# The score products of two query blocks taken together, their second halves on 64 rows of the array each

## Chip, cores and metric

The kernel runs on one core of a Trainium2 chip. The metric is device time in microseconds (us) of one execution. TensorE does the matrix products, ScalarE (ACT) the activations and copies with a scale, VectorE (DVE) the element-wise work and the scans, GpSimd (POOL) small odd jobs, and SyncE (SP) issues most of the DMA transfers.

## What is computed

A transformer block over 2048 tokens of width 1024. Half of its mixing is stick-breaking attention with 8 heads of 64 channels, the other half is a gated unit; an MLP of width 4096 follows. The change touches the scores `z` of the attention and the store of the queries that feed them.

```python
def stick_breaking_attention(q, k, v):
    # A[t,s] = sigmoid(z_ts) * prod_{s<j<t} (1 - sigmoid(z_tj)), z = q.k / sqrt(Dh)
    for blk in range(s // Q_BLOCK):                 # 128 queries at a time
        qb, kb, vb = qh[:, :, q0:kv_len], kh[:, :, :kv_len], vh[:, :, :kv_len]
        z = jnp.einsum('bhqd,bhkd->bhqk', qb, kb) * scale
        causal = s_idx < t_idx
        log_keep = jnp.where(causal, jax.nn.log_sigmoid(-z), 0.0)
        suffix = lax.cumsum(log_keep, axis=3, reverse=True) - log_keep
        a = jnp.where(causal, jnp.exp(jax.nn.log_sigmoid(z) + suffix), 0.0)
        outs.append(jnp.einsum('bhqk,bhkd->bhqd', a, vb))

x = x + concat(rmsnorm(attention), rmsnorm(gated)) @ w_out
x = x + square(relu(rmsnorm(x) @ w_up)) @ w_down
return rmsnorm(x)
```

## The kernel before

The products are wanted at float32 accuracy, but run in the faster form float32r. So an operand is split by `split` (L85, L86 or L88, L89) into a high part, a rounded copy made by ACT, and a low part, the rest, made by DVE. A product of two split operands is then high x high + high x low + low x high: `mm3` (L93, L94, L95), three matmuls of 512 columns each.

The scores are made in another way. A head has 64 channels, half of the 128 rows of the array, so the tile `qt` holds the high parts of the queries in rows 0 to 63 and their low parts in rows 64 to 127, while `kt` holds the keys twice, once in each half of the rows: `kt[:, 0]` the high parts, `kt[:, 1]` the low parts. One matmul over 128 rows with `kt[:, 0]` gives high x high and low x high together (L370), and one with `kt[:, 1]` gives high x low and low x low (L371).

The tokens are cut in 4 chunks of 512 (`c`) and these in 4 blocks of 128 queries (`tb`). A unit of the attention is one chunk of queries, one head and one segment of 512 keys (`seg`); there are 80 units and so 320 steps. A step (`weigh`) makes the scores `z` of one query block against up to 512 keys in one of two buffers of the accumulation memory (pool `ps_z`); on the diagonal (`seg == c`, 128 of the steps) the keys are 256, 256, 384 and 512 and a small matmul adds the mask (L373). ACT reads `z` twice (`kk` L377, `b` L379), DVE runs the scan along the keys (L382, L385) and multiplies (L383, L386). Five steps later `turn` transposes `b` on TensorE (L396) and splits it (`aT`, L85, L86), and two steps after that `gather` multiplies it with the values (L414, L415).

The attention is a generator, `side`. The helper `together` runs it beside the main work: one step for each step of the projections of chunks 2 and 3, then half a step for each step of the output projection and of the first MLP half. Where the main work needs a finished chunk of the attention, the attention runs alone until that chunk is there (`while steps[0] < ...: next(side)`). After the attention's end the kernel has the rest of the MLP alone. The order of each engine's instructions is set at build time, by a scheduler that goes by a simulated time line; so an edit in one place can move instructions in others.

The queries come from `transposed_cols(0, q_d)`: 16 results of 128 x 512 are split with one ACT and one DVE instruction each (L88, L89), and stored to `q_d` with two transfers each (L208); `qt` is loaded from there, once for each chunk and head (L359).

Of the kernel before, what the change touches and what calls it, by code (L numbers as in the profile page):

```python
# [8 lines left out]
F32 = mybir.dt.float32  # L9
F32R = mybir.dt.float32r  # L10
# [6 lines left out]
P = 128  # L17
D = 1024
T = 2048
NH = 8  # L20
HD = 64
SBW = 512
DFF = 4096
TC = 512
# [4 lines left out]
QK_SCALE = 0.125  # L29
# [5 lines left out]
def block_kernel(ctx: ExitStack, tc: tile.TileContext, x, x_t, gmix, w_in, ln_g, ln_b, sgw, sgb,  # L35
                 outg, w_out, gmlp, w_up, w_down, gfin, out):
    nc = tc.nc
    const = ctx.enter_context(tc.tile_pool(name="const", bufs=1))
    dram = ctx.enter_context(tc.tile_pool(name="dram", bufs=1, space=DRAM))
# [4 lines left out]
    ident_b = const.tile([P, P], BF16, name="ident_b")  # L44
# [5 lines left out]
    neg_b = const.tile([P, P], BF16, name="neg_b")  # L50
# [12 lines left out]
    nc.gpsimd.memset(mone, -1.0)  # L63


    q_d = dram.tile([NH, 2, HD, T], F32, name="q_d")
    k_d = dram.tile([NH, 2, HD, T], F32, name="k_d")
    v_d = dram.tile([NC, NH, P, NTB, 2, HD], F32, name="v_d")
    a_d = dram.tile([SBW, T], F32, name="a_d")
# [12 lines left out]
    def split(hi, lo, src, scale=None):  # L82

        if scale is None:
            nc.scalar.activation(hi, src, AF.Copy)  # L85
            nc.vector.tensor_tensor(lo, src, hi.bitcast(F32), ALU.subtract)  # L86
        else:
            nc.scalar.activation(hi, src, AF.Copy, scale=scale)  # L88
            nc.vector.scalar_tensor_tensor(lo, src, scale, hi.bitcast(F32), ALU.mult, ALU.subtract)  # L89
# [23 lines left out]
    def proj(cs, places, sp, gated_first, staging):  # L113
# [32 lines left out]
        def weights(col):  # L146
            if col in ready:
                return ready.pop(col)
            return [weight(col, k2) for k2 in range(KD // 2)]
# [37 lines left out]
        def transposed_cols(col, dst):  # L187
            ws = weights(col)
            for ci, (c, pl) in enumerate(zip(cs, places)):
                for e in range(4):  # L190
                    es = slice(e * P, (e + 1) * P)
                    ps = pl.ps()
                    for k in range(KD):
                        w, h = ws[k // 2], hT[ci][k // 2]
                        mm3(ps, w[:, 0, k % 2, es], w[:, 1, k % 2, es], h[:, 0, k % 2, :], h[:, 1, k % 2, :],
                            k == 0, k == KD - 1)
                        if k == 3:
                            yield
                    st = sp.tile([P, 2, TC], F32R, name="qkv_st", bufs=2)
                    if col == 0:  # L200

                        split(st[:, 0, :], st[:, 1, :], ps, QK_SCALE)
                    else:
                        t = sp.tile([P, TC], F32, name="gelu_t", bufs=3)
                        nc.vector.tensor_tensor(t, ps, r_rows[ci], ALU.mult)
                        split(st[:, 0, :], st[:, 1, :], t)
                    for j in range(2):
                        nc.sync.dma_start(dst[2 * e + j, :, :, c * TC:(c + 1) * TC].rearrange("x d t -> d x t"),  # L208
                                          st[j * HD:(j + 1) * HD].bitcast(F32))
                    yield  # L210

        def natural(col, evac):
# [128 lines left out]
    def attention(cs):  # L341

        units = [(c, h, seg) for c in cs for h in range(NH) for seg in range(c, -1, -1)]
        state = {}

        def weigh(u, tb):
            c, h, seg = units[u]
            diag = seg == c
            tcs = slice(c * TC, (c + 1) * TC)
            ss = slice(seg * TC, (seg + 1) * TC)  # L350
            if tb == 0:
                kt = att.tile([P, 2, TC], F32R, name="kt", bufs=2)
                for j in range(2):
                    nc.sync.dma_start(kt[j * HD:(j + 1) * HD].bitcast(F32), k_d[h, :, :, ss].rearrange("x d t -> d x t"))
                vt = att.tile([P, NTB, 2 * HD], F32R, name="vt", bufs=3)
                nc.sync.dma_start(vt.bitcast(F32), v_d[seg, h].rearrange("p n x d -> p n (x d)"))
                if diag:
                    qt = att.tile([P, TC], F32R, name="qt", bufs=2)
                    nc.sync.dma_start(qt.bitcast(F32), q_d[h].rearrange("x d t -> (x d) t")[:, tcs])  # L359
                    carry = [None] * NTB  # L360
                else:
                    qt, carry = state[u - 1][2:4]
                state[u] = [kt, vt, qt, carry, []]
            kt, _, qt, carry, bs = state[u]
            L = (tb + 1) * P if diag else TC
            z = ps_z.tile([P, TC], F32, name="z")
            ql = qt[:, tb * P:(tb + 1) * P]

            Z = max(L, 2 * P)
            nc.tensor.matmul(z[:, :Z], ql, kt[:, 0, :Z], start=True, stop=False)  # L370
            nc.tensor.matmul(z[:, :Z], ql, kt[:, 1, :Z], start=False, stop=not diag)  # L371
            if diag:
                nc.tensor.matmul(z[:, L - P:L], ident_b, neg_b, start=False, stop=True)  # L373
            row = c * NTB + tb
            kk = kks[kk_n[0] % NKK]
            kk_n[0] += 1
            nc.scalar.activation(kk[:, :L], z[:, :L], AF.Sigmoid, scale=rq[:, 1, row:row + 1])  # L377
            b = att.tile([P, TC], F32, name="b", bufs=9)
            nc.scalar.activation(b[:, :L], z[:, :L], AF.Sigmoid, scale=rq[:, 0, row:row + 1])  # L379
            pr = att.tile([P, TC + 1], F32, name="pr", bufs=5)  # L380
            if diag:
                nc.vector.tensor_tensor_scan(pr[:, L - 1::-1], kk[:, L - 1::-1], zeros[:, :L], 1.0, ALU.mult, ALU.add)  # L382
                nc.vector.tensor_tensor(b[:, :L - 1], b[:, :L - 1], pr[:, 1:L], ALU.mult)  # L383
            else:
                nc.vector.tensor_tensor_scan(pr[:, ::-1], kk[:, ::-1], zeros, carry[tb], ALU.mult, ALU.add)  # L385
                nc.vector.tensor_tensor(b, b, pr[:, 1:TC + 1], ALU.mult)  # L386
            carry[tb] = pr[:, 0:1]
            bs.append(b)

        def turn(u, j):  # L390
            c, h, seg = units[u]
            t0 = j * P if seg == c else 0
            bs = state[u][4]
            tr = ps_t.tile([P, TC], F32, name="tr")
            for tb in range(t0 // P, NTB):
                nc.tensor.transpose(tr[:, tb * P:(tb + 1) * P], bs[tb][:, j * P:(j + 1) * P], ident)  # L396
            aT = att.tile([P, 2, TC], F32R, name="aT", bufs=4)
            split(aT[:, 0, t0:], aT[:, 1, t0:], tr[:, t0:])
            if t0 > TC - 2 * P:
                t0 = TC - 2 * P  # L400
                nc.gpsimd.tensor_copy(aT[:, :, t0:t0 + P], zeros[:, :2 * P].rearrange("p (a b) -> p a b", a=2))
            state[u, j] = aT, t0

        heads = {}

        def gather(u, j):
            c, h, seg = units[u]
            first, last = seg == c and j == 0, seg == 0 and j == NTB - 1
            aT, t0 = state.pop((u, j))
            vt = state[u][1]  # L410
            if first:
                heads["av"] = ps_av.tile([P, TC], F32, name="av")
            av = heads["av"]
            nc.tensor.matmul(av[:, t0:], vt[:, j, :], aT[:, 0, t0:], start=first, stop=False)  # L414
            nc.tensor.matmul(av[:, t0:], vt[:, j, :], aT[:, 1, t0:], start=False, stop=last)  # L415
            if not last:
                return
            if h % 2 == 0:
                heads["ao"] = att.tile([P, TC], F32, name="ao", bufs=1)
            ao = heads["ao"]  # L420
            low = att.tile([HD, TC], F32, name="low", bufs=1)
            nc.scalar.activation(low, av[HD:2 * HD, :], AF.Copy)
            o0 = (h % 2) * HD
            nc.vector.tensor_tensor(ao[o0:o0 + HD, :], av[0:HD, :], low, ALU.add)
            if h % 2 == 1:
                nc.sync.dma_start(a_d[(h // 2) * P:(h // 2 + 1) * P, c * TC:(c + 1) * TC], ao)

        n = len(units) * NTB
        for i in range(n + DRAIN):
            if i < n:  # L430
                weigh(i // NTB, i % NTB)
            if 0 <= i - LATE < n:
                turn((i - LATE) // NTB, (i - LATE) % NTB)
            if i >= DRAIN:
                gather((i - DRAIN) // NTB, (i - DRAIN) % NTB)
            steps[0] = i + 1
            yield
# [550 lines left out]
    with ExitStack() as es:  # L988
        att = es.enter_context(tc.tile_pool(name="att", bufs=1, side="right", reuse_waits="tile"))
        ps_z = es.enter_context(tc.tile_pool(name="ps_z", bufs=2, space=PSUM, reuse_waits="tile"))  # L990
# [99 lines left out]
```

## Time and profile before

| what | value |
|---|---|
| median of 3 runs | 2500.56 us (2498.76 to 2502.59) |
| profiled execution, its own time | 2500.81 us |
| span from its first to its last instruction | 2499.1 us |
| granted TensorE clock, mean | 0.985 |
| TensorE matmul busy | 2427.0 us (97%) |
| DVE busy | 1686.5 us (67%) |
| ACT busy | 1197.9 us (48%) |

In the rows below PE is TensorE's matmuls, PEld its loads of the stationary operand (the weights) and SPq the queue in which SyncE issues transfers. L370 is line 370 of the kernel before. Busy times of PE are modelled ends of pipelined instructions and overlap: what a matmul takes from the engine is read from the distance between the starts of two that follow one another.

### The profile page before, as it was taken

The numbers are of one execution on the slowest core, as the hardware profiler recorded it, in microseconds if no ns is written. First come the engines' busy times: TensorE is split into PE (matmuls) and PEld (weight loads), VectorE is DVE, ScalarE is ACT, GpSimd is POOL, SyncE is SP. The second block draws the span as 40 slices with busy tenths as digits, with TensorE's granted clock in tenths as the row PEclk, the third lists the DMA queues.
The fourth block names the chain that finished last, engine by engine and source line by source line (L and its number), as shares of the span: only waits on it lengthen the run. The fifth ranks groups of instructions, "written<-read, shape, count | busy, mean of one in ns | idle before, by whom it ended". The sixth has DMA issues, their size and how long they took to land.

```text
span 2499.1 us, 30545 instructions
## 1 busy us (share of the span) xinstructions
PE 2427.0 (97%) x11424; PEld 1986.8 (79%) x11424; DVE 1686.5 (67%) x2264; ACT 1197.9 (48%) x2004; POOL 322.1 (13%) x288
## 2 busy tenths in 40 slices
PE   8999999998899999999999899999999999899998
PEld 7888788886687888888877688888888888688886
DVE  4752678865957666666668878744686666577788
ACT  5433457553736655655655545322244444433333
POOL 1110011000100000000000000000123222224432
PEclk9999999998999999999989999999999999999999
DMA  9788977668644334433364543353533444744422
GB/s 378 295 303 280 316 256 247 200 217 282 199 148 143 119 125 131 122 115 111 124 257 170 176 130 113 105 197 126 211 118 139 155 146 163 260 182 153 168 101 101
DMA packets 161108, 455.00 MB, mean 182 GB/s; under 512 B 13376, under 2 KB 29760, under 8 KB 141504
## 3 DMA queue, kind: packets, MB, share of 16 engines
q1 hardware_dynamic: 150320, 417.39, 49.3%
q0 software_dynamic: 6336, 33.56, 3.3%
q10 hardware_dynamic: 4304, 2.10, 0.3%
q8 instruction: 90, 1.47, 0.2%
q14 instruction: 58, 0.48, 0.1%
HBM read 322.97 MB, written 130.02 MB: 181 GB/s over the span
## 4 chain that ended last, share of the span: by engine, by line
PE 83%; DVE 8%; DMA 4%; issue 3%; ACT 2%; POOL 0%; SPq 0%; DVEq 0%; POOLq 0%; ACTq 0%
PE mm L94 23%; PE mm L95 23%; PE mm L93 23%; PE tr L396 4%; PE av L414 2%; PE av L415 2%; PE z L370 2%; PE z L371 2%; DVE w L86 2%; DMA v_d<-qkv_st 1%; DVE pr L385 1%; DMA w_in<-wi_d 1%; PE mm L524 1%; DVE t L86 1%; DVE aT L86 1%
## 5 line engine op out<-in xcount | busy, mean ns | idle before, releaser
L93 PE MATMUL mm<-t,t 128*128 128x512 f32 x1280 | 503.7, 395 | 1.4 <-DVE t L86 1.4
L95 PE MATMUL mm<-t,t 128*128 128x512 f32 x1280 | 503.1, 393 | 0.0
L94 PE MATMUL mm<-t,t 128*128 128x512 f32 x1280 | 501.8, 392 | 0.0
L377 ACT ACTIVATE kk<-z,rq 128x512 f32<-128x512 f32 (+2 forms) x320 | 201.7, 631 | 289.0 <-PE z L371 177.0
L385 DVE TENSOR_TENSOR_SCAN pr<-kk,pr,zeros 128x513 f32<-128x513 f32 x192 | 246.6, 1285 | 119.1 <-ACT kk L377 118.7
L93 PEld LDWEIGHTS mm<-t,t 128*128 128x128 f32 x1280 | 242.3, 189 | 52.0 <-DVE t L86 1.9
L95 PEld LDWEIGHTS mm<-t,t 128*128 128x128 f32 x1280 | 241.7, 189 | 51.8
L94 PEld LDWEIGHTS mm<-t,t 128*128 128x128 f32 x1280 | 242.0, 189 | 50.1
L85 ACT ACTIVATE aT<-tr 128x512 fp32r<-128x512 f32 (+1 forms) x320 | 172.1, 541 | 100.2 <-PE tr L396 99.5
L86 DVE TENSOR_TENSOR aT<-tr,aT 128x512 fp32r<-128x512 f32 (+1 forms) x320 | 190.7, 599 | 25.3 <-ACT aT L85 25.2
L396 PE MATMUL tr<-ident,b 128*128 128x128 f32 x1088 | 180.9, 279 | 24.2 <-DVE aT L86 21.9
L379 ACT ACTIVATE b<-z,rq 128x512 f32<-128x512 f32 (+2 forms) x320 | 201.0, 629 | 2.8 <-PE tr L396 2.7
L85 ACT ACTIVATE t<-t 128x1024 fp32r<-128x1024 f32 x104 | 104.5, 1059 | 170.4 <-DMA t<-in_w_down 101.3
L94 PE MATMUL mm<-w,w 128*128 128x512 f32 x448 | 176.3, 393 | 8.8 <-DVE w L86 8.6
L396 PEld LDWEIGHTS tr<-ident,b 128*128 128x128 f32 x1088 | 133.2, 143 | 60.7 <-DVE aT L86 30.4
L95 PE MATMUL mm<-w,w 128*128 128x512 f32 x448 | 175.1, 391 | 0.0
L85 ACT ACTIVATE w<-raw 128x512 fp32r<-128x512 f32 (+1 forms) x135 | 106.7, 802 | 140.4 <-PE mm L95 130.7
L382 DVE TENSOR_TENSOR_SCAN pr<-kk,zeros 128x128 f32<-128x128 f32 (+3 forms) x128 | 104.4, 818 | 92.0 <-ACT kk L377 91.8
L86 DVE TENSOR_TENSOR w<-raw,w 128x512 fp32r<-128x512 f32 (+1 forms) x135 | 149.9, 1112 | 0.9 <-ACT w L85 0.4
L95 PE MATMUL mm<-t,w 128*128 128x512 f32 x380 | 150.3, 396 | 0.0
L93 PE MATMUL mm<-t,w 128*128 128x512 f32 x380 | 150.2, 395 | 0.0
L94 PE MATMUL mm<-t,w 128*128 128x512 f32 x380 | 150.2, 395 | 0.0
(215 smaller groups left out, 4730.8 us busy)
## 6 DMA issues: line engine op xcount, KB each, us to landing
w_in<-wi_d SPq DMA_DIRECT2D x40, 1024.0 KB, 8.5
kt<-k_d SPq DMA_DIRECT2D x160, 256.0 KB, 5.0
t<-wo_d SPq DMA_DIRECT2D x32, 1024.0 KB, 8.9
t<-in_w_down SPq DMA_DIRECT2D x28, 1024.0 KB, 7.1
raw<-s_d SPq DMA_DIRECT2D x28, 1024.0 KB, 4.8
wi_d<-w_in POOLq DMA_DIRECT2D x20, 1024.0 KB, 10.3
vt<-v_d SPq DMA_DIRECT2D x80, 256.0 KB, 2.7
t<-in_w_up SPq DMA_DIRECT2D x16, 1024.0 KB, 7.6
```

The lines of the kernel that those rows point to most:

```text
L85: nc.scalar.activation(hi, src, AF.Copy)
L86: nc.vector.tensor_tensor(lo, src, hi.bitcast(F32), ALU.subtract)
L93: nc.tensor.matmul(ps, lh, rh, start=first, stop=False, skip_group_check=more)
L94: nc.tensor.matmul(ps, lh, rl, start=False, stop=False, skip_group_check=more)
L95: nc.tensor.matmul(ps, ll, rh, start=False, stop=last, skip_group_check=more)
L370: nc.tensor.matmul(z[:, :Z], ql, kt[:, 0, :Z], start=True, stop=False)
L371: nc.tensor.matmul(z[:, :Z], ql, kt[:, 1, :Z], start=False, stop=not diag)
L377: nc.scalar.activation(kk[:, :L], z[:, :L], AF.Sigmoid, scale=rq[:, 1, row:row + 1])
L379: nc.scalar.activation(b[:, :L], z[:, :L], AF.Sigmoid, scale=rq[:, 0, row:row + 1])
L382: nc.vector.tensor_tensor_scan(pr[:, L - 1::-1], kk[:, L - 1::-1], zeros[:, :L], 1.0, ALU.mult, ALU.add)
L385: nc.vector.tensor_tensor_scan(pr[:, ::-1], kk[:, ::-1], zeros, carry[tb], ALU.mult, ALU.add)
L396: nc.tensor.transpose(tr[:, tb * P:(tb + 1) * P], bs[tb][:, j * P:(j + 1) * P], ident)
```

## The change

Two query blocks are handled in one go, in the even steps. Their first products run as before over 128 rows, one after the other, into both buffers of `z` (L384 of the changed kernel; the masks, L386, follow each). Of the second product only high x low is kept. It needs 64 rows: for the even block the upper half of the array, for the odd block the lower half (L389), and the two stand next to each other in the code. So that the odd block's high part lies in the lower rows, its `qt` holds low over high. `q_d` is laid out in four planes for that, the queries are split in two instructions of 256 columns instead of one of 512, and stored with four transfers instead of two. ACT, DVE and all that follows in a step are as before.

```diff
-    q_d = dram.tile([NH, 2, HD, T], F32, name="q_d")
+    q_d = dram.tile([NH, 4, HD, T // (2 * P), P], F32, name="q_d")
...
-                        split(st[:, 0, :], st[:, 1, :], ps, QK_SCALE)
+                        blocks = [x.rearrange("p (b a t) -> p b a t", b=2, a=2) for x in (st[:, 0, :], st[:, 1, :])]
+                        for b in range(2):
+                            split(blocks[0][:, b], blocks[1][:, b],
+                                  ps.rearrange("p (a b t) -> p b a t", a=2, b=2)[:, b], QK_SCALE)
...
+                        if col == 0:
+                            qa = dst[2 * e + j, :, :, 2 * c:2 * c + 2].rearrange("q d a t -> d q (a t)")
+                            for i, part in enumerate((qa[:, 0:4:3], qa[:, 1:3])):
+                                nc.sync.dma_start(part, sj[:, i, :].rearrange("d (b t) -> d b t", b=2))
...
-                    qt = att.tile([P, TC], F32R, name="qt", bufs=2)
-                    nc.sync.dma_start(qt.bitcast(F32), q_d[h].rearrange("x d t -> (x d) t")[:, tcs])
+                    qt = att.tile([P, 2, 2 * P], F32R, name="qt", bufs=2)
+                    nc.sync.dma_start(qt.bitcast(F32), q_d[h, :, :, 2 * c:2 * c + 2]
+                                      .rearrange("(b x) d a t -> (x d) b (a t)", b=2))
...
-            z = ps_z.tile([P, TC], F32, name="z")
-            ql = qt[:, tb * P:(tb + 1) * P]
-
-            Z = max(L, 2 * P)
-            nc.tensor.matmul(z[:, :Z], ql, kt[:, 0, :Z], start=True, stop=False)
-            nc.tensor.matmul(z[:, :Z], ql, kt[:, 1, :Z], start=False, stop=not diag)
-            if diag:
-                nc.tensor.matmul(z[:, L - P:L], ident_b, neg_b, start=False, stop=True)
+            if tb % 2 == 0:
+
+                zs.clear()
+                for n in (tb, tb + 1):
+
+                    Ln = (n + 1) * P if diag else TC
+                    zs.append((ps_z.tile([P, TC], F32, name="z"), max(Ln, 2 * P)))
+                    z, Z = zs[-1]
+                    nc.tensor.matmul(z[:, :Z], qt[:, n % 2, n // 2 * P:(n // 2 + 1) * P], kt[:, 0, :Z], start=True, stop=False)
+                    if diag:
+                        nc.tensor.matmul(z[:, Ln - P:Ln], ident_b, neg_b, start=False, stop=False)
+                for n, (z, Z) in zip((tb, tb + 1), zs):
+                    half = slice(n % 2 * HD, (n % 2 + 1) * HD)
+                    nc.tensor.matmul(z[:, :Z], qt[half, n % 2, n // 2 * P:(n // 2 + 1) * P], kt[half, 1, :Z], start=False, stop=True)
+            z = zs[tb % 2][0]
```

What the scheduler makes of it on TensorE is shown at two places. The first is off the diagonal, amid the first MLP half (`mm` are its matmuls, `tr` and `av` those of `turn` and `gather`). Before, the first block's scores stand there alone, and the second block's some 20 rows later:

```order
L95 MATMUL mm_9765<-t8_5871,t8_9760 128x512
L370 MATMUL z_9816<-kt_9811,qt_9375 128x512 [waits DMAHW1_49,DMAHW0_49,Activation_49]
L371 MATMUL z_9816<-kt_9811,qt_9375 128x512
L396 MATMUL tr_9825<-ident_60,b_9531 128x128 [waits DVE_49]
L396 MATMUL tr_9825<-ident_60,b_9565 128x128
```

In the changed kernel both blocks' scores stand together at this place, and the second buffer is waited for as well:

```order
L96 MATMUL mm_9832<-t8_5933,t8_9827 128x512
L384 MATMUL z_9880<-kt_9875,qt_9439 128x512 [waits DMAHW7_49,DMAHW6_49,Activation_49]
L384 MATMUL z_9882<-kt_9875,qt_9439 128x512 [waits Activation_49]
L389 MATMUL z_9880<-kt_9875,qt_9439 128x512
L389 MATMUL z_9882<-kt_9875,qt_9439 128x512
L431 MATMUL av_9714<-aT_9816,vt_9589 128x512 [waits Activation_49]
```

The four score matmuls moved into one run, with the two of 64 rows (L389) next to each other. In 110 of the 160 pairs the two L389 stand so; in the other 50 the scheduler put other work between them. Such a place is on the diagonal, during the projection of chunk 2. Before:

```order
L93 MATMUL mm_2436<-hT_1883,w_in_2206 128x512
L370 MATMUL z_2381<-kt_2374,qt_2379 128x256 [waits DMAHW4_49,DMAHW3_49,DMAHW5_49,PE_49,Activation_49]
L371 MATMUL z_2381<-kt_2374,qt_2379 128x256
L373 LDWEIGHTS ident_b_65
L373 MATMUL z_2381<-neg_b_70,ident_b_65 128x128
L94 MATMUL mm_2436<-hT_1883,w_in_2206 128x512
```

And in the changed kernel:

```order
L384 MATMUL z_2421<-kt_2414,qt_2419 128x256 [waits DMAHW4_49,DMAHW3_49,DMAHW5_49,PE_49,Activation_49]
L386 LDWEIGHTS ident_b_65
L386 MATMUL z_2421<-neg_b_70,ident_b_65 128x128
L389 MATMUL z_2421<-kt_2414,qt_2419 128x256
L94 MATMUL mm_2480<-hT_1915,w_in_2238 128x512
L95 MATMUL mm_2480<-hT_1915,w_in_2238 128x512
L96 MATMUL mm_2480<-hT_1915,w_in_2238 128x512
L94 MATMUL mm_2480<-hT_1922,w_in_2240 128x512
L95 MATMUL mm_2480<-hT_1922,w_in_2240 128x512
L96 MATMUL mm_2480<-hT_1922,w_in_2240 128x512
L384 MATMUL z_2424<-kt_2414,qt_2419 128x256 [waits PE_49,Activation_49]
```

Here only the mask moved ahead of the second product; each L389 of 64 rows stands alone between matmuls of 128 rows.

## Rows read from the trace of the kernel before

**Rows 1.** The page's first part: busy us (share of the span) and instructions.

```profile
PE 2427.0 (97%) x11424; PEld 1986.8 (79%) x11424; DVE 1686.5 (67%) x2264; ACT 1197.9 (48%) x2004; POOL 322.1 (13%) x288
```

**Rows 2.** Stretches: length, busy PE, PEld, DVE, ACT, POOL, granted clock, DMA share, GB/s.

```profile
255.00:560.00 305.00, 303.99 (x1569) 249.51 (x1567) 229.41 (x384) 169.45 (x338) 25.05 (x29) 1.00 0.75 247
560.00:770.00 210.00, 183.60 (x907) 147.79 (x907) 152.30 (x229) 108.16 (x209) 16.36 (x22) 0.93 0.63 206
770.00:1280.00 510.00, 509.81 (x2530) 421.27 (x2528) 332.02 (x425) 310.28 (x551) 11.04 (x14) 1.00 0.41 128
1280.00:1400.00 120.00, 104.59 (x494) 83.60 (x495) 92.74 (x126) 64.17 (x117) 6.24 (x7) 0.89 0.68 231
1400.00:1620.00 220.00, 220.00 (x1061) 181.53 (x1060) 170.21 (x218) 100.80 (x159) 1.79 (x2) 1.00 0.34 105
```

**Rows 3.** The same view, for instructions on `z` alone (PE, PEld, ACT).

```profile
255.00:560.00 305.00, 47.86 (x222) 29.83 (x164) 83.28 (x162) 1.00 0.75 247
770.00:1280.00 510.00, 75.33 (x284) 46.83 (x248) 144.03 (x246) 1.00 0.41 128
1400.00:1620.00 220.00, 23.17 (x84) 14.35 (x76) 47.17 (x80) 1.00 0.34 105
```

**Rows 4.** Timeline of PE around two steps' scores: start us, duration us, instruction.

```profile
1102.06 0.39 PE L370 MATMUL z<-kt,qt 128*128 128x512 f32 x1
1102.29 0.39 PE L371 MATMUL z<-kt,qt 128*128 128x512 f32 x1
1102.52 0.39 PE L414 MATMUL av<-aT,vt 128*128 128x512 f32 x1
...
1103.21 0.40 PE L95 MATMUL mm<-t,t 128*128 128x512 f32 x1
1103.45 0.60 PE L396 MATMUL tr<-ident,b 128*128 128x128 f32 x4
1103.80 0.48 PE L415 MATMUL av<-aT,vt 128*128 128x512 f32 x1
1104.12 0.39 PE L93 MATMUL mm<-t,t 128*128 128x512 f32 x1
...
1106.17 0.28 PE L370 MATMUL z<-kt,qt 128*128 128x256 f32 x1
1106.29 0.28 PE L371 MATMUL z<-kt,qt 128*128 128x256 f32 x1
1106.41 0.23 PE L373 MATMUL z<-neg_b,ident_b 128*128 128x128 bf16 x1
1106.47 0.61 PE L396 MATMUL tr<-ident,b 128*128 128x128 f32 x4
```

**Rows 5.** Timeline of PEld at the same place.

```profile
1102.06 0.19 PEld L371 LDWEIGHTS z<-kt,qt 128*128 128x128 f32 x1
1106.42 0.42 PEld L396 LDWEIGHTS tr<-ident,b 128*128 128x128 f32 x4
```

**Rows 6.** Timeline of ACT at the same place.

```profile
1103.30 0.68 ACT L379 ACTIVATE b<-z,rq 128x512 f32<-128x512 f32 x1
```

**Rows 7.** Who waited for whom: us in total, times, longest us.

```profile
PE tr L396 <- DVE aT L86: 21.9, 21, 3.7
```

**Rows 8.** Groups by line and shape: busy us, mean ns of one, idle before.

```profile
L377 ACT ACTIVATE kk<-z,rq 128x512 f32<-128x512 f32 x224 | 155.7, 696 | 203.4 <-PE z L371 177.0 <-PE z L373 24.0 <-DVE pr L385 1.5
L377 ACT ACTIVATE kk<-z,rq 128x256 f32<-128x256 f32 x32 | 15.4, 481 | 34.7 <-PE z L373 34.7
```

**Rows 9.** Timeline of SP's queue and PE where the last queries are stored.

```profile
234.22 1.23 SPq L208 DMA_DIRECT2D q_d<-qkv_st  x2
236.79 0.33 SPq L138 DMA_DIRECT2D w_in<-wi_d  x1
...
245.06 0.47 PE L93 MATMUL mm<-hT,w_in 128*128 128x512 f32 x1 [0.44 <-DMA w_in<-wi_d]
```

More of the change, by code (lines that the diff above doesn't have):

```diff
@@ L207, in transposed_cols @@
                     for j in range(2):
-                        nc.sync.dma_start(dst[2 * e + j, :, :, c * TC:(c + 1) * TC].rearrange("x d t -> d x t"),
-                                          st[j * HD:(j + 1) * HD].bitcast(F32))
+                        sj = st[j * HD:(j + 1) * HD].bitcast(F32)
+                        if col == 0:
+                            qa = dst[2 * e + j, :, :, 2 * c:2 * c + 2].rearrange("q d a t -> d q (a t)")
+                            for i, part in enumerate((qa[:, 0:4:3], qa[:, 1:3])):
+                                nc.sync.dma_start(part, sj[:, i, :].rearrange("d (b t) -> d b t", b=2))
+                        else:
+                            nc.sync.dma_start(dst[2 * e + j, :, :, c * TC:(c + 1) * TC].rearrange("x d t -> d x t"), sj)
                     yield
@@ L344, in attention @@
         state = {}
+        zs = []
         def weigh(u, tb):
@@ L348, in weigh @@
             diag = seg == c
-            tcs = slice(c * TC, (c + 1) * TC)
             ss = slice(seg * TC, (seg + 1) * TC)
```

## The prediction

> **What bounds the kernel now.** I read the page's first part, then the busy time by stretch, then the timeline of TensorE inside one stretch, then the waits. TensorE's matmuls are busy 97% of the span [rows 1], but that is a mean over stages, so the stretches come next [rows 2]. The attention, and with it every score, lies between 255 and 1620 us. In three stretches (255 to 560, 770 to 1280, 1400 to 1620 us, together 1035 us) PE is busy 304.0 of 305, 509.8 of 510 and 220 of 220 us, at the full granted clock, while DVE has 170.2 of 220 us in the fullest and ACT 310.3 of 510 us in its fullest. Busy PE is not yet full PE, since the modelled ends overlap: so the reader looks at the starts [rows 4]. At 1102.06, 1102.29 and 1102.52 us three matmuls of 512 columns start 0.23 us apart and nothing stands between them, though each is shown as 0.39 us long; this goes on through the stretches. These three stretches are thus a closed row of matmuls, and a matmul taken out of them shortens the kernel by the distance of its starts. The other two stretches (560 to 770 and 1280 to 1400 us) have PE idle for 26.4 and 15.4 us, and a clock of 0.93 and 0.89: there the attention runs alone to catch up and PE waits, mostly for DVE (the transposes for `aT`, 21.9 us in 21 waits [rows 7]). A matmul taken out there buys nothing, and I count nothing for it.
>
> **How many pairs lie in the full stretches.** Each step loads weights for L370 and L371, so the weight loads on `z` [rows 3] count the steps: 164 / 2 = 82, 248 / 2 = 124 and 76 / 2 = 38, that is 41, 62 and 19 pairs, 122 of the 160. I assigned the pairs of the changed order to these stretches by their number: the two matmuls of 64 rows are neighbours in 26, 54 and 16 of them, 96 in all, and apart in 26. Among the 96, the narrower one has 512 columns in 61 pairs, 384 in 20 and 256 in 15.
>
> **What is removed.** For a pair before, L371 runs twice over the full array; if two neighbours on different halves run at the same time, one of these goes. The price of 512 columns is the 0.23 us of the starts, of 256 columns 0.12 us (1106.17, 1106.29, 1106.41) [rows 4], of 384 by the straight line between them 0.175. The sum is 61 x 0.23 + 20 x 0.175 + 15 x 0.12 = 14.0 + 3.5 + 1.8 = **19.3 us** at most. The 26 pairs that stand apart remove nothing: a matmul over 64 rows has as many columns to stream. In the waiting stretches the order leaves 17 more neighbours of 38 pairs; at most 2.7 us, counted as nothing, kept for the lower end.
>
> **What is added on TensorE: a change of the array's form.** A neighbouring pair changes from 128 rows to 64 and back, 2 changes; a pair apart has 4. In the full stretches that is 96 x 2 + 26 x 4 = **296 changes**. No row of before has a matmul over 64 rows, so their price is bounded. From below by the changes that there are: four transposes between products, 1103.21 to 1104.12 us [rows 4], take 0.91 us in all; two products of 0.23 and four transposes at the rate of their weight loads (0.42 us for four [rows 5]) make 0.46 + 0.42 = 0.88, so 0.03 us is left for two changes, 0.015 each. The bf16 mask, 128 columns between float32 products, takes 0.06 us from start to start (1106.41 to 1106.47), half of what 256 columns take, so its two changes show nothing. Below zero there is no reason for it. From above: if the array must first be empty, a matmul begins when the one before has ended, 0.39 us after its start and not 0.23, so 0.16 us a change; and if the weights, too, can only then be loaded, 0.19 us more [rows 5], 0.35. I take **0.03 us**: the rows near by are those of the lower end (the same engine, another form of instruction between products), and I double theirs, since the split of the rows is a larger change than any of them. That is 296 x 0.03 = 8.9 us given back. The end points are 4.4, 47 and 104 us.
>
> The Trainium skill has two rules on this. Its page "TensorE: Matmul & The Clock Gate" (Part 3, Packing small matmuls) says that matmuls on different row groups run concurrently, some 4 ns apart; no run here shows it yet, and by it the 19.3 us stand whole. Its page "TensorEngine Tiling (Array Packing)" (Key Properties) says that changing the tiling mode drains TensorE; no figure stands there, no row here shows it, and by it the upper prices above are the right ones. It is the first rival.
>
> **What is added as waits.** The second buffer of `z` is now wanted a step earlier: the first matmul into it waits for the `b` of the step just before, not of the one before that. Queued behind it on PE is everything, the main matmuls too. In the trace, the first block of a pair starts at 1106.17 us, and the `b` of the step before ended at 1103.30 + 0.68 = 1103.98 us [rows 4, 6]: 2.2 us to spare. This is the median of the 62 pairs of that stretch; 3 of them are short, by 3.8 us together. In the other two full stretches 5 and 3 pairs are short, by 5.4 and 4.6 us. So 13.8 us if all else stays, and 0 if ACT goes ahead as it can, since it now has the odd block's scores a step earlier (it waited 177.0 us for L371 before [rows 8]). Since the scheduler already moved the worst of them apart, I take 2 us.
>
> **What is added around the queries.** 16 results are split in two instructions of 256 columns instead of one of 512. By ACT's rows for `kk` that is 2 x 0.481 - 0.696 = 0.27 us more each, 4.3 us on ACT and about as much on DVE [rows 8]; both have over 75 us idle in the first full stretch [rows 2], which hides it. Without that cover it is some 4 us. The stores are 64 instead of 32 transfers, 0.62 us each on SP's queue [rows 9], 20 us in all; behind them stand the loads of `w_in`, `kt` and `qt`. In the place where it is tightest, two stores of 1.23 us are followed by 1.3 us until the load of `w_in` that PE then waits 0.44 us for; two more stores just fit. I take 1 us, between 0 and 3. Loads of `qt` have pieces of half the size and as many bytes: nothing.
>
> **The sum.** -19.3 + 8.9 + 2 + 1 = -7.4 us. The profiled execution took 2500.81 us (its span is 2499.1), 0.25 us over the median of the runs; so 2500.8 - 7.4 = **2493.4 us**. A measurement of this kernel can tell about 0.2%, 5 us, from no change. With a change of form at 0.015 and no waits the time is 2500.8 - 19.3 + 4.4 = 2486; at 0.05, with the 3 us, it is 2499. So this case alone spans 2485 to 2501.
>
> **Rivals.**
> - *The array empties at each change.* The mechanism is in the full stretches, at L389 and at the matmul behind it: 296 x 0.16 = 47 us against 19.3, with the 3 us of waits and stores +31, **2532 us**. The point from which the change loses is 16.3 / 296 = 0.055 us a change. For it: a matmul's shown length of 0.39 us against 0.23 between starts says that much is under way when the next begins, and the two forms must not mix in one buffer of `z`, which the first product and the second both add to. Against it: the changes among transposes, mask and products cost 0.015 us. That TensorE drains at such a change is what the tiling page of the Trainium skill states.
> - *It empties and then loads weights.* 296 x 0.35 = 104 us, +87, **2588 us**. For it: the load of L371, at 1102.06 us, stands under the matmul of L370 [rows 4, 5], and that cover would be gone. Against it: all that the first rival has against it, and that loads of another form (bf16 mask) ran ahead here.
> - *The halves run one after the other.* The change does not do what it says: the weight load of the lower half begins only when the upper half's matmul does, as the load of L371 begins with the matmul of L370 [rows 4, 5], and takes 0.19 of the 0.23 us. The 19.3 us shrink to 3.4; with 8.9 us for the changes and the 3 us the time is **2509 us**, with changes at 0.015 2505. For it: no load in the trace begins before the matmul ahead of the one it serves. Against it: those are all loads of the same 128 rows, and these are not.
> - *The wait for the second buffer.* The 13.8 us come in full: -19.3 + 8.9 + 13.8 + 1 = +4.4, **2505 us**, from level to slightly slower.
>
> **How the numbers follow.** Forecast 0.50 (0.42 faster by over 0.2%, 0.08 within); the array empties 0.20 (slower); empties and loads 0.09 (slower); one after the other 0.12 (0.05 within, 0.07 slower); the wait 0.09 (0.05 within, 0.04 slower). Together faster 0.42, same 0.18, slower 0.40. Cases of both signs are likely, so the forecast's own range is 2485 to 2501. The range for 8 in 10 leaves out the 0.09 of the dearest case and a little at each end: from 2477 (all 19.3 us, and the 2.7 us and a little more in the waiting stretches, with free changes) to 2540 (the emptied array with more of the waits).
>
> **What would show it.** In the trace after, the starts of two neighbouring L389: a few ns apart says concurrent, 0.19 says that the loads follow one another, 0.23 that nothing is shared. The distance from the second L384 to the first L389, less 0.23, and from the last L389 to the next matmul, is the price of a change, 0.03 by my step. PE waits on ACT `b` at L384 show the second buffer. The length of the three full stretches must shrink by 7 us together; if they shrink but the two waiting stretches grow, the order is to blame. I am wrong if a change costs over 0.055 us.

## The result and the profile after

The changed kernel takes 2542.9 us (median of 4 runs, 2539.0 to 2544.4), beside 2499.7 us (median of 4) for the kernel before: a ratio of 1.017, with a 95% interval of 1.015 to 1.019. It is **43 us slower**. The forecast was 7 us faster, and the time lies 3 us above the range.

The first lines of the page answer to [rows 1]. PE now has 58 us more busy time; DVE has what it had, and ACT 4 us more, as much as the prediction has for the split of the queries:

```profile
span 2542.7 us, 30647 instructions
PE 2485.0 (98%) x11424; PEld 1978.7 (78%) x11424; DVE 1685.9 (66%) x2280; ACT 1201.9 (47%) x2020; POOL 320.6 (13%) x288
```

The lines of the second products, before (L371) and after (L389), with duration min/median/max in ns and the first and last start, show two things. The median is 497 ns where it was 392, though as many columns are streamed. And the last one starts at 1625.4 us, where the last L371 started at 1588.0: 37 of the 43 us have been lost by the end of the scores.

```profile
L371 PE MATMUL z<-kt,qt x320: 274/392/628, 258.6 to 1588.0; 128*128 128x512 f32 x96, 128*128 128x256 f32 x32, 128*128 128x384 f32 x32
L389 PE MATMUL z<-kt,qt x320: 379/497/792, 257.8 to 1625.4; 64*128 64x512 f32 x96, 64*128 64x256 f32 x32, 64*128 64x384 f32 x32
```

Where they go is to be seen in the timeline of PE at a pair in the full stretch, which answers to [rows 4] (start us, duration us, instruction; "x2" stands for two merged):

```profile
1121.26 0.40 PE L96 MATMUL mm<-t,t 128*128 128x512 f32 x1
1121.49 0.62 PE L384 MATMUL z<-kt,qt 128*128 128x512 f32 x2
1122.04 0.50 PE L389 MATMUL z<-kt,qt 64*128 64x512 f32 x2
1122.47 0.50 PE L431 MATMUL av<-aT,vt 128*128 128x512 f32 x1
1122.81 0.39 PE L94 MATMUL mm<-t,t 128*128 128x512 f32 x1
1123.04 0.39 PE L95 MATMUL mm<-t,t 128*128 128x512 f32 x1
```

- The two L389 take 0.50 us together, and one alone is 0.497 long: they start at the same time to the hundredth (3 to 4 ns apart in the trace) and **do run at once**. (The two L384 take 0.62: 0.39 and a start 0.23 later.)
- The second L384 starts at 1121.49 + 0.23 = 1121.72. The halves start 0.32 us later, not 0.23: **0.09 us** are lost.
- The next matmul starts 0.43 us after the halves, which stream for 0.23: another 0.20 us.
- The one after that starts 0.34 us later: 0.11 us.

So 0.40 us are lost for this excursion into 64 rows and back, 0.20 for each of its two changes. It is the price where a product of 512 columns stands behind the halves. Behind 79 of the 110 neighbouring pairs there is a transpose. There the first two losses are the same, but the matmul behind the first transpose comes after 0.164 us where it came after 0.109 before (medians over the traces): 0.055 us are lost at this place and 0.35 in all.

The weight loads (PEld) at the same place show the kind of loss, beside [rows 5]:

```profile
1121.26 0.42 PEld L384 LDWEIGHTS z<-kt,qt 128*128 128x128 f32 x2
1122.04 0.19 PEld L389 LDWEIGHTS z<-kt,qt 64*128 64x128 f32 x2 [0.35 <-issue]
1122.47 0.19 PEld L431 LDWEIGHTS av<-aT,vt 128*128 128x128 f32 x1 [0.25 <-ACT t L627]
1122.58 0.19 PEld L94 LDWEIGHTS mm<-t,t 128*128 128x128 f32 x1
```

In [rows 5] the load for L371 starts with the matmul ahead of it. Here the loads of the halves do not start at 1121.72 with the second L384, but at 1122.04 with the halves themselves, and that of L431 starts at 1122.47 with L431. A load no longer stands under the matmul ahead when the number of rows changes. (The trace puts the second of these waits down to an ACT instruction; the same gap stands before `tr` and `mm` and in runs where no such instruction is near, so that is a coincidence.) I read the 0.40 us as twice 0.09 until the array may change over, and twice 0.11 of a weight load that is no longer hidden (0.055 where the load is that of a transpose, which is shown as 0.14 us long and not 0.19). That is a reading of the starts; experiments 5 and 7 test it.

The sum with 0.20 us a change is 296 x 0.20 = 59.2 us lost and 19.3 us saved in the full stretches. With the 3 us for waits and stores that is +43 us on the 2500.8 us, 2543.7 us; the profiled execution took 2544.4. That it comes out so near is in part luck, as the stretches show. Both kernels have the same main matmuls in the same order, so the stretches of [rows 2] can be bounded by the same matmul in both traces (starts in us):

| stretch | before | changed | longer by |
|---|---|---|---|
| full | 255.1 to 557.0 | 254.1 to 570.8 | 14.8 |
| waiting | 557.0 to 770.1 | 570.8 to 792.1 | 8.2 |
| full | 770.1 to 1278.8 | 792.1 to 1315.1 | 14.3 |
| waiting | 1278.8 to 1400.1 | 1315.1 to 1438.8 | 2.4 |
| full | 1400.1 to 1620.2 | 1438.8 to 1661.4 | 2.5 |

The full stretches have lost 31.6 us, and the waiting ones, for which the prediction and the sum count nothing, another 10.6. With the 19.3 us saved, the 31.6 are 0.17 us for each of the 296 changes, the waits included, and not 0.20, which fits the transposes behind most pairs. In the first waiting stretch the granted clock is also lower than before (the last but two of the figures, 0.93 and 0.89; the first line is the kernel before):

```profile
557.00:770.10 213.10, 186.68 (x924) 150.05 (x923) 154.98 (x232) 110.71 (x214) 16.36 (x22) 0.93 0.62 204
570.80:792.10 221.30, 204.02 (x922) 156.25 (x921) 153.87 (x231) 110.44 (x214) 16.68 (x22) 0.89 0.60 199
```

How much of the 8.2 us the clock makes there, and how much the 64-row matmuls, is not shown.

### The profile page after: what moved, and what is told of

The parts are those of the page before. It is cut to its first block, busy times and chain, and to the rows that moved or that the text cites. A ratio compares the mean times of both kernels' runs of the same rounds, so it can differ in the third digit from the quotient of the medians.

```text
span 2542.7 us, 30647 instructions
## 1 busy us (share of the span) xinstructions
PE 2485.0 (98%) x11424; PEld 1978.7 (78%) x11424; DVE 1685.9 (66%) x2280; ACT 1201.9 (47%) x2020; POOL 320.6 (13%) x288
## 4 chain that ended last, share of the span: by engine, by line
PE 82%; DVE 8%; DMA 5%; issue 2%; ACT 1%; POOL 0%; SPq 0%; POOLq 0%; DVEq 0%; ACTq 0%
PE mm L95 22%; PE mm L94 22%; PE mm L96 22%; PE tr L413 4%; PE z L389 3%; PE av L431 2%; PE z L384 2%; PE av L432 2%; DVE w L87 2%; DVE pr L402 1%; PE mm L541 1%; DMA v_d<-qkv_st 1%; DMA w_in<-wi_d 1%; DMA stx<-in_x_t 1%; DVE t L87 1%
## 5 line engine op out<-in xcount | busy, mean ns | idle before, releaser
L418 POOL CAST aT<-zeros 128x256 fp32r<-128x256 f32 x32 | 27.6, 863 | 987.5 <-PE av L432 959.4
L96 PE MATMUL mm<-t,w 128*128 128x512 f32 x380 | 150.3, 396 | 0.0
L94 PE MATMUL mm<-t,w 128*128 128x512 f32 x380 | 150.2, 395 | 0.0
```

The source lines that it names most:

```text
L94: nc.tensor.matmul(ps, lh, rh, start=first, stop=False, skip_group_check=more)
L96: nc.tensor.matmul(ps, ll, rh, start=False, stop=last, skip_group_check=more)
```

## The experiments

The theory, as it stood before these runs, is a price of 0.20 us for every change, paid in the full stretches alone. The rivals are that the pairs as such, their waits or the stores of the queries make the loss, and that the 64-row matmuls are slow in themselves. The number of changes in each kernel is counted in its built order, in the three full stretches.

**1. The same kernel with full rows.** One line differs, and the built order of TensorE is the same, row for row:

```diff
-  nc.tensor.matmul(z[:, :Z], qt[half, n % 2, n // 2 * P:(n // 2 + 1) * P], kt[half, 1, :Z], start=False, stop=True)
+  nc.tensor.matmul(z[:, :Z], qt[:, n % 2, n // 2 * P:(n // 2 + 1) * P], kt[:, 1, :Z], start=False, stop=True)
```

> The changed kernel, but the second product of each block runs over all 128 rows, as before the change; pairs, layout and stores of the queries and the order of all instructions stay as changed. Theory (a change between 128 and 64 rows costs 0.20 us, 296 of them in the three full stretches): 2543 - 296 x 0.20 + 19.3 = 2503 us, that is the time of before plus the 3 us for waits and stores. Rival (the pairs, the wait for the second buffer or the stores of the queries make the 43 us): it stays at 2540 us or rises by the 19 us of work that comes back, to 2562.

Measured: 2506 us, ratio to the kernel before 1.002 (1.0004 to 1.0036). The loss is gone, though the 19 us of matmuls are back. The timeline of PE shows the pair without gaps, each distance 0.23 us or twice that:

```profile
1094.81 0.62 PE L384 MATMUL z<-kt,qt 128*128 128x512 f32 x2
1095.27 0.61 PE L389 MATMUL z<-kt,qt 128*128 128x512 f32 x2
1095.72 0.39 PE L431 MATMUL av<-aT,vt 128*128 128x512 f32 x1
1095.95 0.40 PE L94 MATMUL mm<-t,t 128*128 128x512 f32 x1
```

So the pairs, the wait for the second buffer and the new stores together cost 1 to 9 us, and the form of the matmul makes the rest. The single runs of this kernel spread from 2495 to 2514 us, wider than those of before (2498 to 2504), and they go with the mean granted clock of each run: 0.990 in the fastest, 0.980 in the slowest, 0.982 to 0.986 in those of before. Why the clock varies more here is not settled. The runs of the changed kernel have 0.981 to 0.984, so a few of its 43 us may be the clock's.

**2. The form without the pairs.** The kernel before, with the second product of each block on the upper 64 rows alone:

```diff
-  nc.tensor.matmul(z[:, :Z], ql, kt[:, 1, :Z], start=False, stop=not diag)
+  nc.tensor.matmul(z[:, :Z], ql[0:HD], kt[0:HD, 1, :Z], start=False, stop=not diag)
```

> The kernel before with one edit: the second product of each block runs over the upper 64 rows only, each alone amid matmuls of 128 rows, no pairs, queries stored as before. All 244 steps in the full stretches then have two changes, 488, and nothing is saved. Theory: 2500 + 488 x 0.20 = 2598 us (some less where ACT or DVE wait anyway). Rival (pairs, waits or stores): 2500 us, since none of them is there. Rival (64-row matmuls are slow in themselves, 0.1 us each, and changes are free): 2500 + 24 = 2524 us.

Measured: 2592 us, ratio 1.036 (1.035 to 1.038). That is 92 us, near the 98 expected, but not all of it lies where the 488 changes are: bounded as in the table above, the full stretches are 75 us longer than before (325.0, 548.5 and 232.7 us), 0.155 us a change, and the waiting ones, with 160 more changes, 13 us. The same steps, here 0.33 and 0.43 us, stand at a half without a neighbour. The product behind the single transpose then comes after 0.08 us; before, it came after 0.03:

```profile
1130.14 0.39 PE L370 MATMUL z<-kt,qt 128*128 128x512 f32 x1
1130.47 0.50 PE L371 MATMUL z<-kt,qt 64*128 64x512 f32 x1
1130.90 0.33 PE L396 MATMUL tr<-ident,b 128*128 128x128 f32 x1
1130.98 0.48 PE L93 MATMUL mm<-t,t 128*128 128x512 f32 x1
```

On the diagonal the bf16 mask stands behind the half; there the matmul behind the mask comes after 0.066 us, as before, and the excursion loses 0.09 + 0.20 = 0.29 us (medians). So the price is 0.29 to 0.40 us, by what stands behind. It does not need a pair, and it is more than the 0.1 us of the rival with slow matmuls. A price for each 64-row matmul would fit this run as well; experiment 6 tells the two apart.

**3. Fewer changes: full rows on the diagonal.**

```diff
-  half = slice(n % 2 * HD, (n % 2 + 1) * HD)
+  half = slice(0, P) if diag else slice(n % 2 * HD, (n % 2 + 1) * HD)
```

> The changed kernel, but the second products on the diagonal run over all 128 rows; the 64 rows are left to the pairs off the diagonal. In the full stretches the order then has 162 changes in place of 296, and 61 pairs that save 0.23 us each. Theory: 2500.8 - 14.0 + 162 x 0.20 + 3 = 2522 us. Rival (a fixed cost of the pairs and their waits): 2543 us, as the changed kernel, or more.

Measured: 2529 us, ratio 1.010 (1.008 to 1.013), between the two and 7 us above the sum, which counts nothing in the waiting stretches; in the trace these are 12 us longer than before. The single runs go from 2519 to 2531, the fastest at a granted clock of 0.987, the others at 0.982 to 0.984. The pairs off the diagonal, the best case of the change, still lose.

**4. No pair parted.** Both buffers become one tile of two banks:

```diff
+  z2 = ps_z.tile([P, 2, TC], F32, name="z", bufs=1)
...
-  zs.append((ps_z.tile([P, TC], F32, name="z"), max(Ln, 2 * P)))
+  zs.append((z2[:, n % 2, :], max(Ln, 2 * P)))
```

> The changed kernel with both score buffers made one tile of two banks, so that both become free together and the scheduler has no reason to part the two matmuls of 64 rows: all 160 pairs are neighbours, 244 changes in the full stretches in place of 296, and 122 pairs save 23.8 us in place of 19.3. Theory: 2500.8 - 23.8 + 244 x 0.20 + 1 = 2527 us, and up to 14 us more for the wait for the odd step's ACT, which now holds both buffers: 2527 to 2541. If the parted pairs were all of the loss (26 in the full stretches), it would be below 2500 us.

Measured: 2526 us, ratio 1.009 (1.007 to 1.011), as the theory has it without further waits. So keeping the pairs together gains 17 of the 43 us; with every pair side by side the change still costs 26 us.

**5. Weights that load faster.** The halves take bf16 operands, an identity and zeros; high x low is missing from the scores.

```diff
-  nc.tensor.matmul(z[:, :Z], qt[half, n % 2, n // 2 * P:(n // 2 + 1) * P], kt[half, 1, :Z], start=False, stop=True)
+  nc.tensor.matmul(z[:, :Z], ident_b[half, :], zero_b[half, :Z], start=False, stop=True)
```

> The changed kernel with the matmuls of 64 rows on bf16 operands (an identity and zeros): they leave high x low out of the scores, so the run is read for its time alone. Their weight load is shown half as long in the trace (0.10 against 0.19 us for the mask's identity). The order has 290 changes in the full stretches, 145 entries into the 64-row form. Theory (a change is 0.09 us until the array is empty and 0.11 us of a weight load that no longer hides): the load at each entry shrinks by some 0.06 us, so about 9 us below the changed kernel, 2534 us, and in the trace the matmul behind the halves starts 0.37 us after them in place of 0.43. Rival (a change is a fixed price of the switch, whatever is loaded): 2543 us and 0.43 us.

Measured: 2523 us, ratio 1.010 (1.008 to 1.012): 20 us below the changed kernel, twice what was expected. In the timeline of PE and PEld the matmul behind the halves comes after 0.32 us, not 0.37:

```profile
1108.76 0.62 PE L386 MATMUL z<-kt,qt 128*128 128x512 f32 x2
1109.31 0.10 PEld L391 LDWEIGHTS <-ident_b 64*128 64x128 bf16 x2 [0.35 <-issue]
1109.31 0.39 PE L391 MATMUL z<-zero_b,ident_b 64*128 64x512 bf16 x2
1109.63 0.50 PE L433 MATMUL av<-aT,vt 128*128 128x512 f32 x1
1109.96 0.40 PE L94 MATMUL mm<-t,t 128*128 128x512 f32 x1
```

The 0.11 us at the entry are gone altogether: 145 entries make 16 us, and the rest is within the spread of the runs. The way into the halves (1108.99 to 1109.31, 0.09 too long), the way out (0.32, again 0.09 too long) and the load of the float32 weights behind them (0.33, 0.10 too long) are unchanged. So the price has two parts, and one of them goes with the operands' type. That it is the load of the weights is argued and not shown by this run alone, since the moving operand is bf16 too. For it speaks that the part shrinks with the shown length of the load: 0.11 us at a load of 0.19, 0.055 at the 0.14 of a transpose, nothing at 0.10. Why a bf16 load, shown with half the length, leaves nothing at all is open.

**6. More work per excursion.** Each 64-row matmul is issued twice; high x low counts twice in the scores.

```diff
-  for n, (z, Z) in zip((tb, tb + 1), zs):
-      half = slice(n % 2 * HD, (n % 2 + 1) * HD)
-      nc.tensor.matmul(z[:, :Z], qt[half, ...], kt[half, 1, :Z], start=False, stop=True)
+  for last in (False, True):
+      for n, (z, Z) in zip((tb, tb + 1), zs):
+          half = slice(n % 2 * HD, (n % 2 + 1) * HD)
+          nc.tensor.matmul(z[:, :Z], qt[half, ...], kt[half, 1, :Z], start=False, stop=last)
```

> The changed kernel with each 64-row matmul issued twice (high x low is counted twice, so it is read for its time alone): four halves in a row where the pair stands together. 282 changes in the full stretches in place of 296. Theory (the price is at the change, and neighbours inside the form run two at a time at 0.23 us for 512 columns): 2543 + 23.8 - 2.8 = 2564 us, and one more pair lengthens a group by 0.23 us. Rival (every 64-row matmul waits for its own weights, 0.1 to 0.2 us): 2543 + 24 + 122 x 0.2 to 0.4 = 2590 us or more.

Measured: 2566 us, ratio 1.027 (1.025 to 1.029), 23 us above the changed kernel, as the theory has it. Four halves last 1114.38 - 1113.72 = 0.66 us, where two last 0.43:

```profile
1113.17 0.62 PE L384 MATMUL z<-kt,qt 128*128 128x512 f32 x2
1113.72 0.73 PE L390 MATMUL z<-kt,qt 64*128 64x512 f32 x4
1114.38 0.55 PE L414 MATMUL tr<-ident,b 128*128 128x128 f32 x3
```

Inside the form a second pair costs only its columns, 0.23 us, and its weights load under the first. The price is at the change.

**7. A bf16 matmul on the way out.** The kernel of experiment 4 with the masks behind the halves:

```diff
-                    if diag:
-                        nc.tensor.matmul(z[:, Ln - P:Ln], ident_b, neg_b, start=False, stop=False)
...
+                if diag:
+                    for n, (z, Z) in zip((tb, tb + 1), zs):
+                        nc.tensor.matmul(z[:, n * P:(n + 1) * P], ident_b, neg_b, start=False, stop=True)
```

> The kernel with both score buffers in one tile, with the two masks of the diagonal moved behind the two halves, so that the first matmul after a diagonal pair has bf16 weights. 41 + 62 + 20 pairs in the full stretches, some 50 of them on the diagonal. Theory (0.11 us of each change is a float32 weight load that no longer hides; a bf16 load hides): 50 x 0.11 = 5 us below the 2526 us of the one-tile kernel, 2520 us, and in the trace the matmul behind the mask starts as after a full matmul. Rival (the price is the switch alone): 2526 us.

Measured: 2524 us, ratio 1.011 (1.009 to 1.012): by the time no different from experiment 4, so inconclusive there. In the trace the part that was asked for is right:

```profile
1062.18 0.50 PE L388 MATMUL z<-kt,qt 64*128 64x384 f32 x2
1062.62 0.28 PE L391 MATMUL z<-neg_b,ident_b 128*128 128x128 bf16 x2
1062.74 0.61 PE L415 MATMUL tr<-ident,b 128*128 128x128 f32 x4
```

The two masks take 0.12 us, 0.06 each, as the one in [rows 4]: no load is left to see behind the halves. That the time shows so little has a reason in the traces: in experiment 4, transposes stand behind 41 of 61 diagonal pairs (those at full clock), where only 0.055 us is lost in place of 0.11; and where a 512-column product stands behind the masks here, the matmul behind it comes after 0.32 us and not 0.23, as if a mask of 0.06 us did not hide its float32 load. That leaves some 2 or 3 us of the 5 (an estimate from these gaps), which the spread of the runs covers.

**8 to 10. Four blocks at a time.** By experiment 6, a group of n pairs of 512 columns loses up to 0.40 us and saves 0.23 n, so two pairs should about break even. That needs four score buffers. They come from the main products (2 for 3) and the transposes (1 for 2), so three kernels share these buffers: four blocks in one tile, pairs in two tiles, and the kernel before. In all three the projection ahead of the attention also takes one more of its results from a sixth buffer of its second pool (`ps_x`). The edit, cut:

```diff
-  ps_mm ... bufs=3; ps_t ... bufs=2; ps_z ... bufs=2
+  ps_mm ... bufs=2; ps_t ... bufs=1; ps_z ... bufs=4
...
-  if tb % 2 == 0:
+  if tb == 0:
+      z4 = ps_z.tile([P, NTB, TC], F32, name="z", bufs=1)
```

> The changed kernel with all four query blocks of a unit taken together in one tile of four score buffers (the other pools give up two: 2 buffers for the main products, 1 for the transposes). The order then has 173 changes in the full stretches, many runs of three and four halves, some parted by the scheduler. Theory (a run of halves costs 0.40 us however long it is, and each pair in it saves 0.23): 173 x 0.20 - some 20 = +15 us over the kernel before with the same buffers, and 14 us below the pairs with the same buffers. It would pay only if no run were parted: 122 changes, 24 - 24 = 0. Rival (the price is by the matmul of 64 rows): as the pairs.

> The changed kernel's pairs with the buffers of the four-block kernel (two tiles of two score buffers). 258 changes in the full stretches, nearly all pairs neighbours. Theory: 258 x 0.20 - 23.5 = +28 us over the kernel before with the same buffers.

> The kernel before with the buffers of the two kernels above and no 64-row matmul: what the buffers alone do. Between 2500 us (four score buffers help, the lost ones were not needed) and some 20 us more (products or transposes wait for their one or two buffers).

Measured: 2888, 2846 and 2801 us, ratios 1.156, 1.140 and 1.121 to the kernel before with its own buffers. The buffers alone cost 303 us (against 2498.3 on the same chip), far over the 20 us that I had as the worst. The attention falls behind the main work: its last L371 starts at 1969.6 us, where it started at 1588.0 before. PE waits longer for `aT` than before, where the first of these lines had 21.9 us [rows 7] and the second 1.0 (the kernel before with these buffers; who waited for whom, us in total, times, longest us):

```profile
PE tr L396 <- DVE aT L86: 52.4, 43, 3.1
PE av L414 <- ACT aT L85: 35.5, 66, 5.1
```

The mean granted clock of that run is 0.933 against 0.985. Against it the pairs lose 44 us (28 expected) and the four blocks 86 us (15 expected). Four blocks have fewer changes than the pairs and are 42 us slower. A waiting line differs, PE `z` on ACT `b`, 33.1 us in 24 waits with four blocks and 15.5 us in 31 waits with pairs, but that alone does not make 42 us; the granted clock differs too, 0.910 and 0.924, and the shares are not told apart. Since in these kernels PE is no longer a closed row of matmuls, they say nothing on the price of a change, and whether longer groups pay where buffers are free stays open. No version here beats the kernel before.

## Why the prediction was wrong, point by point

- **What bounds the kernel** was right for the full stretches: 31.6 us are lost there. But what happens to the scores in the waiting stretches was counted as nothing, and these are 10.6 us longer. The sign that I gave, full stretches shorter by 7 us together, did not come.
- **What is removed** was right: the halves run at once when they are neighbours, and a pair saves one matmul, 0.23 us for 512 columns. Experiment 4 against the changed kernel fits the 122 pairs.
- **The change of the array's form is the step that failed.** I took 0.03 us for each of the 296 changes. It is up to 0.20 and on average 0.17 (waits included), which turns the 8.9 us of that term into some 50 us. I had chosen the value by the rows nearest at hand, transposes and masks between products, and these change the instruction, but not the number of rows. They were the wrong neighbour, and no row of before has the right one, a matmul over 64 rows. The point from which I called the change lost, 0.055 us, was exceeded three times over.
- **The bounds** of that price, 0.015 and 0.35 us, held it. The first rival (0.16 us, 2532 us, chance 0.20) and the second (0.35 us, 2588 us, chance 0.09) had the two right parts with wrong sizes: the wait at the change is 0.09 us and not 0.16 (the next matmul starts before the shown end of the last, after 0.32 us of its 0.39), and the load adds up to 0.11 us and not 0.19. The truth lies between them, and my range closed at 2540, short of it; it should have run on to the second rival. The rule of the Trainium skill on the first rival (page "TensorEngine Tiling (Array Packing)", Key Properties: a change of tiling mode drains TensorE) agrees with what the trace shows, 0.09 us at each change. The Trainium skill's rule on concurrent row groups (page "TensorE: Matmul & The Clock Gate", Part 3) agrees too: 0.50 us for two L389 of 0.497.
- **A row was misread.** Against the second rival I held that the load of the bf16 mask ran ahead. It starts at 1106.40 us, with its matmul (1106.41 in [rows 4]) and not with the one ahead of it (1106.29):

```profile
1106.17 0.19 PEld L371 LDWEIGHTS z<-kt,qt 128*128 128x128 f32 x1
1106.40 0.10 PEld L373 LDWEIGHTS <-ident_b 128*128 128x128 bf16 x1
```

  So this row said that a bf16 load costs nothing even where it does not run ahead, as experiment 5 found, and nothing of float32 loads.
- **The halves in turn** did not happen: both weight loads stand within the 0.19 us of one.
- **The wait for the second buffer** and **the stores** came to 1 to 9 us in experiment 1; the sum had 3. In the profile after, PE waits 1.9 us in 3 waits for `b` at L384, less than the 5.7 us before.

## What to carry to other kernels

Two matmuls on different halves of the array's rows do run at once, but going to 64 rows and back costs 0.29 to 0.40 us here, by what stands behind, and no more with two pairs together (experiment 6). That is more than the one 512-column matmul (0.23 us) that a pair saves. So count the excursions, not the matmuls: by these prices such packing can pay only where at least two pairs stand in one run, or where a whole stage stays in the form. No run here shows a gain. When a price stands in no row, the range must reach to its upper bound, and a row of another kind of change is no estimate of it.

## What the runs showed of the hardware

- A change between matmuls over 128 and over 64 rows stops the weight loads from running ahead: the load starts with its matmul (1122.04 us for both), and the matmul behind then comes 0.11 us late with float32 weights, 0.055 with those of a transpose, 0.00 with bf16 operands (experiment 5).
- The change itself costs 0.09 us in each direction, also where the matmul behind it goes to another bank (`mm` or `av` behind `z`), so it does not come from adding to the same scores.
- The halves' own weights load at the same time: two loads of 64 rows are shown in 0.19 us, the time of one.
- One accumulation buffer less for the transposes and one less for the main products, with two more for the scores, cost 303 us in this kernel (experiment 10); which of them makes it is not shown.
